# Two-layer hybrid attention trunk on Trainium2: in the last head of each attention, transposed blocks also go to the score tiles' PSUM places, some steps move from GpSimd to VectorE, and three groups of the second branch's projection are opened before the last gated rows are there

## The chip, the cores and the metric

The kernel runs on one core of a Trainium2 chip. Its five engines run their own instruction streams side by side and wait for each other through semaphores: TensorE (PE in the profile; PEld is its weight load), VectorE (DVE), ScalarE (ACT), GpSimd (POOL) and SyncE (SP), from whose queue the DMAs go out. The metric is device time in microseconds, the median of several executions. A profiled execution has its own time, the span from its first instruction to its last.

## The reference, cut to what matters

Two layers. Each normalises 512 latent and 256 context tokens of 1024 channels, projects them, runs two attentions of eight heads of 64 channels beside each other, multiplies each result by its own gate path, projects both to 1024 channels, merges them and projects again. Layer 0 also updates the 256 context tokens, layer 1 the 512 latent tokens alone.

```python
def _attend(q, k, v):
    s = jnp.einsum('bqkgd,btkd->bkgqt', q, k).astype(jnp.float32) * (HEAD_DIM ** -0.5)
    p = jax.nn.softmax(s, axis=-1).astype(v.dtype)
    return jnp.einsum('bkgqt,btkd->bqkgd', p, v)

def _merge(a_att, b_att, a_z, b_z, g_a, g_b, w_o_a, w_o_b, w_out):
    o_a = (a_att * jax.nn.silu(a_z)) @ w_o_a
    o_b = (b_att * jax.nn.silu(b_z)) @ w_o_b
    merged = jax.nn.sigmoid(g_a) * o_a + jax.nn.sigmoid(g_b) * o_b
    return merged @ w_out

# in _layer
    a_att = _na_latent(qa, ka, va, cka, cva, rpb, rows)   # neighbourhood window + all context keys
    b_att = _gqa_latent(qb, k_all, v_all)                 # all 768 keys, 2 key/value heads
    out_x = _merge(a_att, b_att, a_z, b_z, g_a, g_b, w_o_a, w_o_b, w_out)
    x_new = x + gate_x * out_x
```

## The kernel before

**Arithmetic.** Every product of two float32 matrices is made of three matmuls on a high and a low half of each operand (`mm3`, L339 to L343: high by high on L341, the two mixed ones on L342 and L343). A high half is a cast by ScalarE (`pth` L658, `gbh` L543, `whi`), a low half is the rest, left by a subtraction on VectorE or GpSimd (`ptl` L659, `gbl` L544, `wlo`).

**Stages.** Per layer: the projections of keys, queries, values and gates; the neighbourhood attention (NA); the gate path of the second branch; the grouped-query attention (GQ), and beside it, as filling work, the first branch's output projection (`o_a`); then the merge: the second branch's output projection (`o_b`, `w_o_b`) and the last projection with `w_out`. In layer 0 there are 768 tokens, in spans (0:512) and (512:768), in layer 1 only (0:512).

**One attention.** `pipeline` takes the heads in turn: the scores of head h, then the values of head h-1, then some pieces of the filling work. After the scores of head 7 it runs what is left of the filling work and `early`, and the values of head 7. Scores are a product into PSUM (`pss`), a maximum, an exponential on ScalarE, and a normalisation (`softmax_tail`) on GpSimd for tiles 1 and 3 of the four and on VectorE for tiles 0 and 2. The values of a head go block by block (six in GQ, four in NA): four 128x128 transposes of the probabilities into PSUM (`transpose_split`, L653 and L655, tile `pst`), the cast `pth` on ScalarE, the subtraction `ptl` on VectorE, and two or more matmuls into the one value tile `psv` (L807 to L818 in NA, L958 and L959 in GQ). `head_out` then copies and adds the halves of `psv` (`ho`, L667 on ScalarE, L668 on VectorE) and multiplies the gate path's tile by it on GpSimd (L669). In layer 0 a small value product of the context tokens follows each head (L732, L733, in a `psv` of its own).

**Places.** PSUM has two places `t` for transposed blocks (`pst`), one for a projection's sums (`psf`), and what is left depends on the stage: in NA three places `s` for scores (512 columns), in GQ two (1024 columns each), in both one place `v` for `psv`; in the merge five places `x` (`psx`). `pth` and `ptl` have two buffers each (`NT_NA = NT_GQ = 2`). A place is free again when its last reader is done, and the next instruction that writes it waits for that.

**The gated operand of `o_b`.** `zb` holds the gate path multiplied by the attention, four row blocks k = 0 to 3 of two heads each. `hilo(zb, gated["b"], ...)` (L540 to L544) splits them into `gbh` (ScalarE) and `gbl` (GpSimd). Blocks 0 to 2 are split in `early`, before the values of head 7, block 3 (heads 6 and 7) after the pool of the attention is closed. A group of `o_b` (128 output channels by one span of tokens) is four times three matmuls, k = 0 to 3, and its evacuation `evac_b` multiplies the sum by the merge gate (L993), adds (L994), casts (`mh`, L996) and subtracts (`ml`, L997). `gbh` and `gbl` share their large buffers with earlier tiles: in layer 0 `gbl` gets the buffer of `gal`, the low half of the first branch.

**What sets the order.** The program's text gives a first order; a scheduler with a timeline of its own reorders the instructions of each engine at build time, within the dependences. `behind(engine, fn)` ties the instructions of `fn` behind the last one issued so far on that engine.

## Time and profile before

| | |
|---|---|
| time, three runs | 1154.92 us median (1154.86 to 1157.67) |
| span of the profiled execution | 1153.4 us |
| busy: PE, PEld, DVE | 1123.0, 949.0, 809.8 us |
| busy: ACT, POOL | 573.9, 495.0 us |
| PE busy in 883.0 to 893.4 (end of NA, layer 1) | 8.94 of 10.40 us |
| PE busy in 1063.2 to 1084.6 (end of GQ, layer 1) | 18.63 of 21.40 us |
| PE busy in 560.3 to 570.1 (end of GQ, layer 0) | 7.81 of 9.80 us |

NA runs from about 150 to 305 us in layer 0 and from 780 to 893 us in layer 1; GQ from about 305 to 568 us and from 960 to 1084.6 us. The busy time of PE counts pipelined matmuls whose ends are modelled: two in a row start about 0.23 us apart at 512 columns and are listed with 0.39 us each. In a timeline each row is one instruction or several alike: its start, its length, the engine, the line, the operation, what it writes and reads, the tile, the shape, how many; in brackets the idle time ahead of it and what ended it.

### The profile page before, as it was taken

The numbers are of one execution on the slowest core, as the hardware profiler recorded it, in microseconds if no ns is written. First come the engines' busy times: TensorE is split into PE (matmuls) and PEld (weight loads), VectorE is DVE, ScalarE is ACT, GpSimd is POOL, SyncE is SP. The second block draws the span as 40 slices with busy tenths as digits, with TensorE's granted clock in tenths as the row PEclk, the third lists the DMA queues.
The fourth block names the chain that finished last, engine by engine and source line by source line (L and its number), as shares of the span: only waits on it lengthen the run. The fifth ranks groups of instructions, "written<-read, shape, count | busy, mean of one in ns | idle before, by whom it ended". The sixth has DMA issues, their size and how long they took to land.

```text
span 1153.4 us, 17280 instructions
## 1 busy us (share of the span) xinstructions
PE 1123.0 (97%) x6078; PEld 949.0 (82%) x6078; DVE 809.8 (70%) x1508; ACT 573.9 (50%) x1167; POOL 495.0 (43%) x459
## 2 busy tenths in 40 slices
PE   5999999999999999999999999999999999999998
PEld 4688888889988888878788787888888988887786
DVE  4566688897464687688587755469787665898563
ACT  5453266666433465566330265346666445766521
POOL 3362354454375243354411126245553664465311
PEclk9999999999999999999999999999999999999999
DMA  9644222233342332470353523543332333142143
GB/s 368 195 126 137 69 85 65 72 115 97 115 130 63 107 102 73 67 276 19 121 172 101 174 74 110 176 106 113 108 105 84 110 101 101 65 173 92 63 129 92
DMA packets 88000, 134.04 MB, mean 116 GB/s; under 512 B 10629, under 2 KB 52585, under 8 KB 86249
## 3 DMA queue, kind: packets, MB, share of 16 engines
q1 hardware_dynamic: 87912, 132.94, 36.8%
q8 instruction: 48, 0.79, 0.3%
q14 instruction: 40, 0.32, 0.1%
HBM read 115.58 MB, written 17.32 MB: 115 GB/s over the span
## 4 chain that ended last, share of the span: by engine, by line
PE 83%; DVE 7%; issue 3%; POOL 2%; ACT 2%; DMA 2%; ACTq 0%; POOLq 0%; DVEq 0%
PE psx L341 12%; PE psx L343 12%; PE psx L342 12%; PE psf L341 9%; PE psf L342 9%; PE psf L343 9%; PE pst L655 5%; PE pss L704 2%; PE pss L705 2%; PE psv L959 2%; PE psv L958 1%; PE pss L781 1%; PE pst L417 1%; DVE wlo L328 1%; DVE ptl L659 1%
## 5 line engine op out<-in xcount | busy, mean ns | idle before, releaser
L659 DVE TENSOR_TENSOR ptl<-pst,pth 128x512 fp32r<-128x512 f32 (+1 forms) x176 | 116.0, 672 | 46.4 <-ACT pth L658 45.4
L658 ACT CAST pth<-pst 128x512 fp32r<-128x512 f32 (+1 forms) x176 | 99.2, 576 | 87.5 <-PE pst L655 56.3
L328 POOL TENSOR_TENSOR wlo<-raw,whi 128x512 fp32r<-128x512 f32 x68 | 95.0, 1402 | 108.9 <-ACT whi L326 87.8
L341 PE MATMUL psf<-hx,whi 128*128 128x512 f32 (+1 forms) x368 | 139.2, 378 | 0.0
L342 PE MATMUL psf<-hx,whi 128*128 128x512 f32 (+1 forms) x368 | 138.1, 375 | 0.0
L343 PE MATMUL psf<-hx,wlo 128*128 128x512 f32 (+1 forms) x368 | 137.8, 374 | 0.0
L341 PE MATMUL psx<-whi,hx 128*128 128x512 f32 (+1 forms) x368 | 137.2, 374 | 0.0
L342 PE MATMUL psx<-wlo,hx 128*128 128x512 f32 (+1 forms) x368 | 135.8, 369 | 0.0
L343 PE MATMUL psx<-whi,hx 128*128 128x512 f32 (+1 forms) x368 | 133.6, 369 | 0.0
L314 POOL TENSOR_TENSOR wlo<-raw,whi 128x512 fp32r<-128x512 f32 x44 | 60.4, 1373 | 140.4 <-ACT whi L311 123.8
L311 ACT CAST whi<-raw 128x512 fp32r<-128x512 f32 x96 | 58.7, 623 | 103.5 <-PE psx L343 38.6
L326 ACT CAST whi<-raw 128x512 fp32r<-128x512 f32 x136 | 82.5, 622 | 50.3 <-DMA raw<-in_w_in_dram 34.1
L655 PE MATMUL pst<-ident,p 128*128 128x128 f32 x640 | 99.9, 272 | 1.4 <-DVE ptl L659 0.9
L328 DVE TENSOR_TENSOR wlo<-raw,whi 128x512 fp32r<-128x512 f32 x68 | 70.2, 1033 | 28.3 <-ACT whi L326 27.8
L655 PEld LDWEIGHTS pst<-ident,p 128*128 128x128 f32 x640 | 77.7, 141 | 13.3 <-DVE ptl L659 1.6
L644 POOL TENSOR_SCALAR r<-r 128x1 f32<-128x1 f32 x64 | 23.1, 361 | 151.7 <-DVE r L639 144.1
L645 POOL TENSOR_TENSOR p<-p,r 128x512 f32<-128x512 f32 (+1 forms) x64 | 83.5, 1304 | 5.0
L341 PEld LDWEIGHTS psx<-whi,hx 128*128 128x128 f32 x368 | 69.6, 189 | 11.8 <-issue 0.8
L343 PEld LDWEIGHTS psf<-hx,wlo 128*128 128x128 f32 x368 | 69.4, 188 | 11.8
L343 PEld LDWEIGHTS psx<-whi,hx 128*128 128x128 f32 x368 | 69.4, 189 | 11.5
L342 PEld LDWEIGHTS psx<-wlo,hx 128*128 128x128 f32 x368 | 69.6, 189 | 11.0
L341 PEld LDWEIGHTS psf<-hx,whi 128*128 128x128 f32 x368 | 69.4, 189 | 10.8 <-ACT zt L502 0.2
(239 smaller groups left out, 3033.4 us busy)
## 6 DMA issues: line engine op xcount, KB each, us to landing
raw<-in_w_in_dram SPq DMA_DIRECT2D x168, 256.0 KB, 2.9
rawb<-in_w_ada_dram SPq DMA_DIRECT2D x64, 256.0 KB, 2.8
gs<-zt SPq DMA_DIRECT2D x32, 256.0 KB, 2.0
raw<-in_w_out_dram SPq DMA_DIRECT2D x32, 256.0 KB, 2.8
tg<-gs SPq DMA_DIRECT2D x4, 1536.0 KB, 7.4
rawx<-in_w_ada_dram SPq DMA_DIRECT2D x4, 1024.0 KB, 7.2
rawy<-in_w_ada_dram SPq DMA_DIRECT2D x4, 1024.0 KB, 12.2
raw<-in_w_o_a_dram SPq DMA_DIRECT2D x16, 256.0 KB, 2.7
```

The source lines that it names most:

```text
L311: S.copy(hi[:, :n], raw[:, :n])
L314: e.tensor_tensor(lo[:, :n], raw[:, :n], F(hi[:, :n]), ALU.subtract)
L326: S.copy(hi, raw)
L328: lo_eng(i).tensor_tensor(lo, raw, F(hi), ALU.subtract)
L341: T.matmul(ps, lhs[0], rhs[0], start=first, stop=False)
L342: T.matmul(ps, lhs[0], rhs[1], start=False, stop=False)
L343: T.matmul(ps, lhs[1], rhs[0], start=False, stop=last)
L644: G.tensor_scalar(r[:, i:i + 1], r[:, i:i + 1], 0.5, None, ALU.mult)
L645: G.tensor_tensor(p[:, c0:c1], p[:, c0:c1], r[:, i:i + 1].to_broadcast([128, c1 - c0]), ALU.mult)
L655: T.transpose(pt[:, c0:c0 + 128], src, ident)
L658: S.copy(hi[:, n0:n1], pt[:, n0:n1])
L659: V.tensor_tensor(lo[:, n0:n1], pt[:, n0:n1], F(hi[:, n0:n1]), ALU.subtract)
```

## The change

Four edits, all at the end of an attention:

1. `att["end"]` is set ahead of the values of head 7. From then on every second transposed block goes into a score place `s` (so it is named `pss`) and its two halves into buffers of the probability tiles (`p`) in place of `pth` and `ptl`.
2. In the same stretch the last multiplication of `head_out` is on VectorE, and for head 7 the tiles normalised by GpSimd are 0 and 2 where they were 1 and 3 (`pooled`).
3. Within the pool of GQ, after the values of head 7, three groups of `o_b` are opened: the first in `psf`, two in the halves of one score place (`room`). Their matmuls for k = 0 to 2 are tied behind the last matmul of the values. Then `zb`'s block 3 is split, its low half on VectorE, and the three groups get k = 3 and `evac_b`. In layer 0 these groups are channels 0 (both spans) and 1 (first span), in layer 1 channels 0, 1 and 2.
4. The other groups follow in the merge's pool in the plain order of the loop, with their weights loaded two chunks ahead (`need_wb`) where `o_chunks` stood.

```diff
...
         ps = psw(n1 - n0)
-        nk = len(w)
-        for k in range(nk):
+        chan_mm(ps, w, f, a, n0, n1, 0, len(w))
+        evac(f, n0, n1, ps)
+
+    def chan_mm(ps, w, f, a, n0, n1, k0, k1):
+        for k in range(k0, k1):
             hi, lo = a(0, k), a(1, k)
             mm3(ps, (w[k][0][:, 128 * f:128 * f + 128], w[k][1][:, 128 * f:128 * f + 128]),
-                (R(hi[:, n0:n1]), R(lo[:, n0:n1])), k == 0, k == nk - 1)
-        evac(f, n0, n1, ps)
+                (R(hi[:, n0:n1]), R(lo[:, n0:n1])), k == 0, k == len(w) - 1)
 
...
 
-        def hilo(src, dst, fs):
+        def hilo(src, dst, fs, lo=G):
             sv = src.rearrange("p (f n) -> p f n", f=4)
...
                 S.copy(R(dst[0][:, f, :ntok]), sv[:, f, :ntok])
-                G.tensor_tensor(R(dst[1][:, f, :ntok]), sv[:, f, :ntok], dst[0][:, f, :ntok], ALU.subtract)
+                lo.tensor_tensor(R(dst[1][:, f, :ntok]), sv[:, f, :ntok], dst[0][:, f, :ntok], ALU.subtract)
 
...
 
-                pt = psw(512, "t")
+                spare = att["end"] and att["turn"] % 2 == 1
+                att["turn"] += 1
+                pt = psw(512, "s" if spare else "t")
                 for src, c0 in blocks:
...
                         T.transpose(pt[:, c0:c0 + 128], src, ident)
-                hi = att["p"].tile([128, 512], F32R, tag="pth", name=nm("pth"), bufs=att["nt"])
-                lo = att["p"].tile([128, 512], F32R, tag="ptl", name=nm("ptl"), bufs=att["nt"])
+                if spare:
+                    hi, lo = R(p_tile()[:, 0:512]), R(p_tile()[:, 0:512])
+                else:
+                    hi = att["p"].tile([128, 512], F32R, tag="pth", name=nm("pth"), bufs=att["nt"])
+                    lo = att["p"].tile([128, 512], F32R, tag="ptl", name=nm("ptl"), bufs=att["nt"])
                 S.copy(hi[:, n0:n1], pt[:, n0:n1])
...
                 V.tensor_tensor(t1[m:m + 64, :n], po[m:m + 64, :n], t1[m:m + 64, :n], ALU.add)
-                G.tensor_tensor(dst, dst, t1[m:m + 64, :n], ALU.mult)
+                (V if att["end"] else G).tensor_tensor(dst, dst, t1[m:m + 64, :n], ALU.mult)
 
...
 
+            def pooled(tiles):
+                return [i - 1 for i in tiles] if att["h"] == 7 else tiles
+
             def p_tile():
...
                 att["w"], att["np"], att["nt"] = width, n_p, n_t
+                att["end"], att["turn"] = False, 0
                 return st
...
                                  accum_out=r[:, 0:1])
-                    softmax_tail(p, 512, r[:, 0:1], [(0, 512)], G if i in NA_POOL else None)
+                    softmax_tail(p, 512, r[:, 0:1], [(0, 512)], G if i in pooled(NA_POOL) else None)
                     ps_.append(p)
...
                     att["bg"] = bg if h > 3 or pm["n"] == 1 else []
+                    att["h"] = h
                     st = scores_of(h)
...
                 run(bg, len(bg))
+                att["end"] = True
                 values_of(7, prev)
...
                     S.activation(p, pss, AF.Exp, bias=mx[:, 0:1], accum_out=r[:, 0:1])
-                    softmax_tail(p, 768, r[:, 0:1], [(0, 768)], G if i in GQ_POOL else None)
+                    softmax_tail(p, 768, r[:, 0:1], [(0, 768)], G if i in pooled(GQ_POOL) else None)
                     ps_.append(p)
...
             pipeline(fill, 8, gq_first, values_of(zb, gq_values), early, bg)
+            ob, wb, mg = [], {}, []
+            act_b = lambda part, k: gated["b"][part][:, k, :]
+
+            def need_wb(f):
+                for i in range(f // 2, min(f // 2 + 2, 4)):
+                    if i not in wb:
+                        wb[i] = load_w2(w_o_b[l], 256 * i, 4, mix_lo)
+
+            def evac_b(f, n0, n1, ps):
+                a, b = tg_part(0, f, n0, n1), tg_part(1, f, n0, n1)
+                V.scalar_tensor_tensor(b, b, 1.0, ps, ALU.add, ALU.mult)
+                V.tensor_tensor(a, a, b, ALU.add)
+                if f // 4 == len(mg):
+                    mg.append(hilo_tiles("m"))
+                hi, lo = [m[:, f % 4, n0:n1] for m in mg[f // 4]]
+                S.copy(R(hi), a)
+                V.tensor_tensor(R(lo), a, hi, ALU.subtract)
+            groups = [(f, n0, n1) for f in range(8) for n0, n1 in spans]
+            room = psw(1024, "s")
+            for (f, n0, n1), ps in zip(groups, (psw(), room[:, 0:512], room[:, 512:1024])):
+                need_wb(f)
+                ps = ps[:, :n1 - n0]
+                behind(ON_PE, lambda: chan_mm(ps, wb[f // 2], f % 2, act_b, n0, n1, 0, 3))
+                ob.append((f, n0, n1, ps))
+            hilo(zb, gated["b"], [3], V)
+            for f, n0, n1, ps in ob:
+                chan_mm(ps, wb[f // 2], f % 2, act_b, n0, n1, 3, 4)
+                evac_b(f, n0, n1, ps)
             gq_es.close()
...
                 nc.sync.dma_start(gv[:, v, :], src.to_broadcast([128, DM]))
-            hilo(zb, gated["b"], [3])
...
-            chunks = o_chunks("b", None, evac_b)
-            chunks[0][0]()
-            for i in range(4):
-                if i < 3:
-                    chunks[i + 1][0]()
-                if i % 2 == 0:
-                    mg.append(hilo_tiles("m"))
-                for piece in chunks[i][1]:
-                    piece()
+            for f, n0, n1 in groups[len(ob):]:
+                need_wb(f)
+                chan_proj(wb[f // 2], f % 2, act_b, n0, n1, lambda _, a, b, ps, f=f: evac_b(f, a, b, ps))
```

No matmul is added or removed: PE has 5769 instructions in the listed order before and after. VectorE has 8 more, GpSimd 8 fewer.

How the order moves at three places. First PE at the end of NA in layer 1; `psv_9420` are the values of head 6, `psv_9529` those of head 7, `p_9381` and the like its probabilities. Before:

```order
L653 MATMUL pst_9541<-ident,p_9381 128x2x64
L655 MATMUL pst_9541<-ident,p_9391 128x128
L655 MATMUL pst_9541<-ident,p_9402 128x128
L655 MATMUL pst_9541<-ident,p_9412 128x128
L653 MATMUL pst_9552<-ident,p_9381 128x2x64
L655 MATMUL pst_9552<-ident,p_9391 128x128 x2
L655 MATMUL pst_9552<-ident,p_9402 128x128
L807 MATMUL psv_9529<-pth_9535,va_1709_7711 128x512
L808 MATMUL psv_9529<-ptl_9536,va_1709_7711 128x512
L807 MATMUL psv_9529<-pth_9546,va_1709_7711 128x512
L808 MATMUL psv_9529<-ptl_9547,va_1709_7711 128x512
```

Now, where `pss_9540` and `pss_9564` are two of head 7's blocks and `pst_9442` is one of head 6's:

```order
L657 MATMUL pss_9540<-ident,p_9380 128x2x64
L659 MATMUL pss_9540<-ident,p_9391 128x128
L657 MATMUL pss_9564<-ident,p_9380 128x2x64
L659 MATMUL pss_9540<-ident,p_9401 128x128
L659 MATMUL pss_9564<-ident,p_9401 128x128
L659 MATMUL pss_9540<-ident,p_9412 128x128
L659 MATMUL pss_9564<-ident,p_9412 128x128 x2
L657 MATMUL pst_9442<-ident,p_9222 128x2x64
L659 MATMUL pst_9442<-ident,p_9232 128x128 x2
L659 MATMUL pst_9442<-ident,p_9243 128x128
```

Two of head 7's four blocks are transposed before head 6 has its last two; before, all four came after.

Second, PE at the end of GQ in layer 0; `psv_6264` are the values of head 7, `psf_6238` (earlier in the list before) is the last group of `o_a`, `psf_6393` and `psf_6354` are the first group of `o_b`. Before:

```order
L341 MATMUL psf_6393<-gbh_6256,whi_6369 128x512
L958 MATMUL psv_6264<-pth_6314,vb_3447 128x512
L342 MATMUL psf_6393<-gbl_6257,whi_6369 128x512
L343 MATMUL psf_6393<-gbh_6256,wlo_6371 128x512
L341 MATMUL psf_6393<-gbh_6256,whi_6369 128x512
L959 MATMUL psv_6264<-ptl_6315,vb_3447 128x512
L958 MATMUL psv_6264<-pth_6325,vb_3447 128x512
L655 MATMUL pst_6335<-ident,p_6086 128x128 x4
L959 MATMUL psv_6264<-ptl_6326,vb_3447 128x512
L342 MATMUL psf_6393<-gbl_6257,whi_6369 128x512
L343 MATMUL psf_6393<-gbh_6256,wlo_6371 128x512
L341 MATMUL psf_6393<-gbh_6256,whi_6375 128x512
```

Now:

```order
L342 MATMUL psf_6238<-gal_5523,whi_5980 128x256
L343 MATMUL psf_6238<-gah_5522,wlo_5982 128x256
L971 MATMUL psv_6264<-pth_6325,vb_3447 128x512
L972 MATMUL psv_6264<-ptl_6326,vb_3447 128x512
L739 MATMUL psv_6344<-p_6340,vb_3447 128x256
L740 MATMUL psv_6344<-p_6341,vb_3447 128x256
L739 MATMUL psv_6344<-p_6340,vb_3447 128x256
L740 MATMUL psv_6344<-p_6341,vb_3447 128x256
L341 MATMUL psf_6354<-gbh_6256,whi_6357 128x512
L342 MATMUL psf_6354<-gbl_6257,whi_6357 128x512
L343 MATMUL psf_6354<-gbh_6256,wlo_6359 128x512
```

The first `o_b` matmuls stood between head 7's values; now they stand behind all of them, and the last `o_a` group, which came ahead of four blocks of head 7, stands ahead of the last one. VectorE at the same place, from the evacuation of that last `o_a` group on:

```order
L580 SCALAR_TENSOR_TENSOR tg_5534<-tg_5534,psf_6238 128x256
L328 TENSOR_TENSOR wlo_6550<-raw_6546,whi_6548 128x512
L675 TENSOR_TENSOR ho_6331<-psv_6264,ho_6331 64x512
L676 TENSOR_TENSOR zb_4101<-zb_4101,ho_6331 64x512
L675 TENSOR_TENSOR ho_6349<-psv_6344,ho_6349 64x256
L676 TENSOR_TENSOR zb_4101<-zb_4101,ho_6349 64x256
L546 TENSOR_TENSOR gbl_6257<-zb_4101,gbh_6256 128x768
L1002 SCALAR_TENSOR_TENSOR tg_6252<-tg_6252,psf_6354 128x512
```

The first value tile's addition (`ho_6331`) stands behind that evacuation and a weight subtraction (`wlo_6550`); the two gate multiplications (`zb_4101`) and the low half (`gbl_6257`), which were on GpSimd, follow it.

Third, PE in layer 1, at the last product of block 3; `psf_11818`, and now `psf_11779`, is the first open sum. Before, after the values of head 7:

```order
L958 MATMUL psv_11708<-pth_11769,vb_9656 128x512
L959 MATMUL psv_11708<-ptl_11770,vb_9656 128x512
L341 MATMUL psx_11835<-gbh_11700,whi_11794 128x512
L342 MATMUL psx_11835<-gbl_11701,whi_11794 128x512
L343 MATMUL psx_11835<-gbh_11700,wlo_11796 128x512
L341 MATMUL psx_11835<-gbh_11700,whi_11794 128x512
L342 MATMUL psx_11835<-gbl_11701,whi_11794 128x512
L343 MATMUL psx_11835<-gbh_11700,wlo_11796 128x512
```

Now, after the k = 0 to 2 products of the three open sums:

```order
L341 MATMUL psf_11779<-gbh_11699,whi_11788 128x512
L341 MATMUL pss_11778<-gbh_11699,whi_11788 128x512
L342 MATMUL psf_11779<-gbl_11700,whi_11788 128x512
L343 MATMUL psf_11779<-gbh_11699,wlo_11790 128x512
L342 MATMUL pss_11778<-gbl_11700,whi_11788 128x512
L343 MATMUL pss_11778<-gbh_11699,wlo_11790 128x512
L341 MATMUL psf_11879<-gbh_11699,whi_11794 128x512
L342 MATMUL psf_11879<-gbl_11700,whi_11794 128x512
L343 MATMUL psf_11879<-gbh_11699,wlo_11796 128x512
L341 MATMUL psf_11879<-gbh_11699,whi_11794 128x512
```

Before, the values of head 7 are followed by other sums, each in a place of its own; now the fourth group, `psf_11879`, takes the same place as the first as soon as its sum is closed.

8 lines of the change are left out of this document (removed).

## Prediction

> **What bounds the kernel now.** I read the page first, then the table of what PE waited for, then the busy time by stretches, then the timelines of the stretches in which PE stands still. The page:
>
> ```profile
> PE 1123.0 (97%) x6078; PEld 949.0 (82%) x6078; DVE 809.8 (70%) x1508; ACT 573.9 (50%) x1167; POOL 495.0 (43%) x459
> ...
> PE   5999999999999999999999999999999999999998
> ...
> PEclk9999999999999999999999999999999999999999
> ...
> PE 83%; DVE 7%; issue 3%; POOL 2%; ACT 2%; DMA 2%; ACTq 0%; POOLq 0%; DVEq 0%
> ```
>
> PE is busy 97% of the span, its granted clock never falls under nine tenths after the start, and 83% of the chain of waits is PE. The work of PE is not changed: the change can only give or take time in which PE stands still. The table of what PE waited for (total us, times, longest) is led, after the start of the kernel, by waits that belong to the ends of the attentions:
>
> ```profile
> PE psv L959 <- DVE ptl L659: 2.0, 3, 1.5
> PE pst L653 <- DVE ptl L659: 1.5, 3, 0.8
> PE psx L341 <- DVE ho L668: 1.2, 1, 1.2
> ```
>
> They sum to 4.7 us. By stretches, the ends of NA in layer 1, of GQ in layer 1 and of GQ in layer 0 (the first pair of numbers is PE's busy time):
>
> ```profile
> 883.00:893.40 10.40, 8.94 (x55) 6.71 (x55) 6.89 (x12) 5.86 (x12) 3.82 (x4) 1.00 0.02 6
> 1063.20:1084.60 21.40, 18.63 (x98) 13.14 (x98) 13.60 (x20) 11.21 (x20) 9.21 (x8) 1.00 0.20 58
> 560.30:570.10 9.80, 7.81 (x45) 5.98 (x44) 5.21 (x7) 3.27 (x6) 8.79 (x6) 1.00 0.26 80
> ```
>
> PE idles 10.40 - 8.94 = 1.46, 21.40 - 18.63 = 2.77 and 9.80 - 7.81 = 1.99 us there, 6.2 us in all. That, 0.5% of the span, is about all that the change can win. A difference under 0.3% (3.5 us) is taken as no change, since a measurement of this kernel hardly tells it from none.
>
> **The change, end by end.** *NA, layer 1.* The timeline of PE:
>
> ```profile
> 883.15 0.27 PE L653 MATMUL pst<-ident,p 128*128 128x128 f32 x1
> 883.26 0.49 PE L655 MATMUL pst<-ident,p 128*128 128x128 f32 x3
> 884.59 0.33 PE L653 MATMUL pst<-ident,p 128*128 128x128 f32 x1 [0.84 <-DVE ptl L659]
> ...
> 889.44 0.33 PE L653 MATMUL pst<-ident,p 128*128 128x128 f32 x1 [0.27 <-DVE ptl L659]
> ...
> 893.11 0.39 PE L817 MATMUL psv<-ptl,va 128*128 128x256 f32 x1 [0.19 <-DVE ptl L659]
> ...
> 893.43 0.30 PE L341 MATMUL psx<-whi,hx 128*128 128x256 f32 x1
> ```
>
> A block of head 6 waits 0.84 us for a place that a `ptl` still reads; head 7's blocks wait 0.27, and their last products 0.19. VectorE has the reason:
>
> ```profile
> 890.05 0.69 DVE L659 TENSOR_TENSOR ptl<-pst,pth 128x512 fp32r<-128x512 f32 x1
> 891.29 0.62 DVE L659 TENSOR_TENSOR ptl<-pst,pth 128x448 fp32r<-128x448 f32 x1 [0.55 <-ACT pth L658]
> 892.43 0.62 DVE L659 TENSOR_TENSOR ptl<-pst,pth 128x448 fp32r<-128x448 f32 x1 [0.52 <-ACT pth L658]
> ```
>
> With two places, each subtraction follows a cast that follows four transposes that had to wait for the subtraction before: they start 1.24 and 1.14 us apart, with 0.62 to 0.69 us of work. With four places two of head 7's blocks are transposed in the 0.84 us wait (eight transposes, 0.11 us apart as at 883.15 and 883.26, are 0.87 us), and the four subtractions no longer wait in turn. From the other side, VectorE now does two of head 7's subtractions ahead of one of head 6's, which comes some 0.35 us later than it could. The stretch idles 1.46 us: the gain lies between 0 and 1.46, and I take 1.2, near the upper end, since the transposes that fill the wait are work that stood behind it.
>
> *GQ, layer 1.*
>
> ```profile
> 1065.14 0.50 PE L959 MATMUL psv<-ptl,vb 128*128 128x512 f32 x1 [1.54 <-DVE ptl L659]
> ...
> 1078.20 0.66 PE L655 MATMUL pst<-ident,p 128*128 128x128 f32 x4 [0.44 <-DVE ptl L659]
> ...
> 1084.24 0.50 PE L959 MATMUL psv<-ptl,vb 128*128 128x512 f32 x1 [0.22 <-DVE ptl L659]
> 1084.58 0.40 PE L341 MATMUL psx<-gbh,whi 128*128 128x512 f32 x1
> 1084.82 0.39 PE L342 MATMUL psx<-gbl,whi 128*128 128x512 f32 x1
> ...
> 1090.06 0.39 PE L341 MATMUL psf<-gbh,whi 128*128 128x512 f32 x1
> ```
>
> Head 7's last four blocks run from 1078.20 to 1084.58, 6.38 us. Between these rows PE has 12 products, which start 0.23 to 0.24 us apart where nothing waits (1084.58 and 1084.82), and 16 transposes: 12 x 0.23 + 16 x 0.11 = 4.5 us of work, 1.9 us lost. The wait of 1.54 us at 1065.14 belongs to head 6 and stays. The twice as many places take away what is lost, up to 1.9 us; two subtractions and head 6's `ho` addition still queue in a row on VectorE ahead of the second block, about 0.7 us, so I take 1.2. What follows was hidden before: after 1084.58 PE runs open sums without a gap until block 3 is split and k = 3 comes (1090.06), 5.5 us later. Now the three open sums cover the same chain with 27 products, 27 x 0.23 = 6.2 us, so opening them wins nothing in layer 1. Their evacuation is new. The first group's last product and VectorE's evacuations before:
>
> ```profile
> 1091.19 0.39 PE L343 MATMUL psf<-gbh,wlo 128*128 128x512 f32 x1
> ```
>
> ```profile
> 1091.62 0.69 DVE L993 SCALAR_TENSOR_TENSOR tg<-tg,psf 128x512 f32<-128x512 f32 x1 [0.24 <-PE psf L343]
> ...
> 1092.82 1.57 DVE L994 TENSOR_TENSOR tg<-tg,tg 128x512 f32<-128x512 f32 x1
> ...
> 1094.91 0.68 DVE L994 TENSOR_TENSOR tg<-tg,tg 128x512 f32<-128x512 f32 x1
> ```
>
> From the start of a sum's last product to the end of its evacuation it takes 1091.62 - 1091.19 + 0.69 = 1.12 us. The order puts the fourth group, `psf_11879`, into the same place behind two products of the second sum: PE has its own 0.23 and 2 x 0.23 to do, and waits 1.12 - 0.69 = 0.4 to 0.5 us. `psf_12061`, first of the last projection, waits in the same way for the fourth group's evacuation behind three products: 1.12 - 4 x 0.23 = 0.2 us. The first `psx` groups lie where `room` was and wait for its two evacuations, which stand behind a weight subtraction: I put 0.25 us. Together 0.95 us lost. Bounds for this end: a gain of 1.9 where the evacuations hide, a loss of 3 where they pile up (rival B). I take -1.2 + 0.95 = -0.25.
>
> *GQ, layer 0.* PE, GpSimd and VectorE before:
>
> ```profile
> 559.93 0.28 PE L342 MATMUL psf<-gal,whi 128*128 128x256 f32 x1
> ...
> 562.95 0.40 PE L341 MATMUL psf<-gbh,whi 128*128 128x512 f32 x1
> 563.34 0.50 PE L959 MATMUL psv<-ptl,vb 128*128 128x512 f32 x1
> ...
> 565.04 0.40 PE L341 MATMUL psf<-gbh,whi 128*128 128x512 f32 x1
> 566.22 0.50 PE L342 MATMUL psf<-gbl,whi 128*128 128x512 f32 x1 [0.79 <-POOL gbl L544]
> ...
> 568.22 0.28 PE L343 MATMUL psx<-gbh,wlo 128*128 128x256 f32 x1
> 569.70 0.50 PE L341 MATMUL psx<-gbh,whi 128*128 128x512 f32 x1 [1.20 <-DVE ho L668]
> ```
>
> ```profile
> 560.29 4.09 POOL L544 TENSOR_TENSOR gbl<-zb,gbh 128x768 fp32r<-128x768 f32 x2 [3.60 <-PE psf L342]
> ```
>
> ```profile
> 560.37 0.42 DVE L578 SCALAR_TENSOR_TENSOR tg<-tg,psf 128x256 f32<-128x256 f32 x1 [0.22 <-PE psf L343]
> 560.90 1.78 DVE L328 TENSOR_TENSOR wlo<-raw,whi 128x512 fp32r<-128x512 f32 x1
> ...
> 565.88 0.69 DVE L668 TENSOR_TENSOR ho<-psv,ho 64x512 f32<-64x512 f32 x1
> ```
>
> GpSimd does the three low halves `gbl` in one run of 5.87 us. It starts at 560.29, when the last `o_a` product with `gal`, whose buffer it takes, is through (started at 559.93). PE filled these 6.3 us (559.93 to the product at 566.22) with four blocks of head 7 and lost (563.34 - 562.95 - 0.23) + (566.22 - 565.04 - 0.23) = 0.16 + 0.95 us; at 569.70 it waits for the addition ahead of a place that `psv` held, 569.70 - 568.22 - 0.12 = 1.36 us. In all 2.5 us. In the new order the last `o_a` group stands behind all but one of head 7's blocks, so the same 5.87 us start with less to do. From that product on PE has: itself and one more of 256 columns (2 x 0.12), 2 products of the last block (0.46), 4 of the context (0.48), the six of k = 0 and 1 in the first open sum (1.38) and the first of k = 2 (0.23), 2.8 us; the low half of k = 2 comes after 6.3 us. PE stands 3.5 us. The context's products need `psv`, freed by VectorE behind an evacuation of 0.42 and a weight subtraction that takes 1.78 beside GpSimd: with the addition of 0.69 that is about 3.2 us, and the 2.1 us of products behind it still end before 6.3. The wait for the addition (1.36) is gone, since the open sums run meanwhile. The next group in `psf` waits for its evacuation: the same 1.12 us, of which two products of 256 columns and the last one's own step cover 0.4 to 0.5: 0.7. Another 0.1 at the first `psx`. That is 4.3 us against 2.5: a loss of 1.8. Bounds: a gain of 2.5 if GpSimd's run starts as early as before, a loss of 5 if nothing but the stretch behind the last block covers it.
>
> The moved multiplications and low halves (`zb`, `gbl` on VectorE) have no row on VectorE before. Nearest are the addition, 0.69 us, and the subtraction of two buffers beside GpSimd, 1.78; alone I take 0.69, nearest in shape. In layer 0 block 3 is ready some 8 us after the product of 559.93: the first addition at 3.2, the context's products 0.5, its copy, addition and multiplication at most 0.69 each, the cast and the low half of 768 columns 1.5 times 0.69 each. PE needs it at 6.3 + 0.5 (the rest of k = 2) + 9 x 0.12 + 9 x 0.23 (the other two sums) = 9.9 us. So these steps cost nothing with 1.9 us to spare, and 3 x 1.1 - 1.9 = 1.4 us if three of them take 1.78.
>
> *NA, layer 0.* Products of the projections stand between head 7's blocks there and cover them; I take 0, within half a microsecond either way. ScalarE's casts, the weight loads and the DMAs stay as many; the loads of `w_o_b` move ahead by one pool, where SP and ScalarE have room: 0.
>
> **Sum.** -1.2 - 0.25 + 1.8 + 0 = +0.35 us on a span of 1153.4. The median of the runs is 1.5 us over that span, so 1155.3 us.
>
> **Rivals.** *A, the waits go and none comes (faster).* The new order does what it is laid out for: layer 1's two ends lose their idle time, 1.46 + 2.77 = 4.2 us, and GQ in layer 0 comes out even, because GpSimd's run starts early enough. For it: nearly all of that idle time hangs on `ptl`, the very place that is doubled. Against it: 1.54 us are head 6's, and GpSimd's run is tied to the last `o_a` product, which the order sets back. Time 1154.9 - 4.2 = 1150.7.
>
> *B, VectorE beside GpSimd (slower).* The steps that move to VectorE read two buffers, and its evacuations now run while GpSimd makes weights. The subtraction of 1.78 us at 560.90 ran inside GpSimd's 5.87, the addition at 1092.82 took 1.57 where the one at 1094.91 took 0.68. If these steps pay 1 us each in the ends of both GQ: 1.4 us in layer 0 beyond the spare time, on top of the 1.8, and in layer 1 four evacuation steps ahead of the fourth group's (two additions, a weight, a low half), which make `psf_12061` wait 2 to 3 us. Sum 0.35 + 1.4 + 2.5 = 4.25 on top of 1154.9: 1159.2. It decides once more than two of these steps in a row meet GpSimd at work. The Trainium skill, "SBUF — State Buffer", section "Who interferes with whom", says that a VectorE instruction with two inputs in SBUF and a GpSimd one that reads SBUF share a read port, and one blocks the other. The trace agrees: 1.78 against 0.68 us, and no delay for the addition with one input in PSUM at 565.88, 0.69. By that rule every moved step is exposed, and the time would be B's.
>
> *C, the change does nothing.* The sums behind head 7 in layer 1 had no gap, and layer 0 might keep its old waits under new names: 1154.9.
>
> **How the numbers follow.** Forecast 0.44, A 0.25, B 0.25, C 0.06. The forecast's own range is 1153 to 1157.5; the range for 8 in 10 reaches into A and B, 1149.8 to 1160. Faster by over 0.3%: most of A and a little of the forecast, 0.25; slower: most of B and a little more, 0.26; within: 0.49.
>
> **What would show it.** Right: in layer 1 no wait of `psv` or `pst` for `ptl` over 0.2 us in head 7's blocks; a wait of 0.4 us or more of the fourth `psf` group; in layer 0 GpSimd's run of three `gbl` starting behind head 7's fifth block and 3 us or more of PE waits on it. Wrong: no wait on `gbl` in layer 0 (then A); VectorE's gate multiplications and low halves over 1.2 us and waits on them (B); a lower granted clock, or a new gap in the last projection, would put the result outside all three.

## The result, and the profile after

| | before | changed |
|---|---|---|
| time, median of five runs each | 1154.92 us (1154.51 to 1157.67) | 1159.49 us (1156.70 to 1160.60) |
| span of the profiled execution | 1153.4 us | 1157.5 us |
| ratio of the times, over all runs | | 1.0031, 95% interval 1.0018 to 1.0045 |

The changed kernel is slower by some 0.3% (the two medians alone differ by 0.4%); the profiled execution is 4.1 us longer. Its page, with the busy times and the shares of the chain that ended last:

```profile
span 1157.5 us, 17279 instructions
PE 1125.4 (97%) x6078; PEld 950.3 (82%) x6078; DVE 815.9 (70%) x1516; ACT 573.4 (50%) x1167; POOL 484.5 (42%) x451
...
PE 84%; DVE 8%; DMA 2%; ACT 2%; issue 1%; POOL 0%; DVEq 0%; ACTq 0%
```

PE is busy for 2.4 us more than before with the same matmuls (6078 records in both profiles; the 5769 given above is not their number), and the chain leads as before through PE. The longest waits of PE on an end of an attention (total us, times, longest):

```profile
PE psv L739 <- DVE ho L675: 2.6, 1, 2.6
PE psv L972 <- DVE ptl L666: 2.2, 4, 1.4
PE psf L341 <- DVE tg L1002: 1.1, 3, 0.6
...
PE psv L818 <- DVE ho L675: 1.0, 1, 1.0
```

`ptl` had led this table before; now it is the one value place: `psv` waits for the addition `ho` of `head_out`, L675, in three attentions (the third, 0.6 us at the end of GQ in layer 1, is shown below).

To see where the 4.1 us arose I compared the starts of the same instructions (same engine, operation and tiles) of ScalarE, VectorE and GpSimd in both traces: the median shift in a stretch, less that ahead of it. The start of the kernel, up to 140 us, which no edit touches, shifts by 0.5 us here and by 0 to 2 us from run to run, so it is kept apart.

| stretch | forecast | shift |
|---|---|---|
| start, untouched | 0 | +0.5 |
| NA, layer 0 | 0 | +0.1 |
| GQ, layer 0, with the merge | +1.8 | +3.4 |
| NA, layer 1 | -1.2 | -0.6 |
| GQ, layer 1, with the merge | -0.25 | +0.75 |
| sum | +0.35 | +4.1 |

**GQ, layer 0.** The timeline of PE from the last `o_a` product that reads `gal`:

```profile
563.18 0.28 PE L342 MATMUL psf<-gal,whi 128*128 128x256 f32 x1
...
563.65 0.39 PE L972 MATMUL psv<-ptl,vb 128*128 128x512 f32 x1
566.69 0.38 PE L739 MATMUL psv<-p,vb 128*128 128x256 f32 x1 [2.64 <-DVE ho L675]
...
567.44 0.63 PE L341 MATMUL psf<-gbh,whi 128*128 128x512 f32 x1
567.87 0.63 PE L342 MATMUL psf<-gbl,whi 128*128 128x512 f32 x1
...
570.43 0.39 PE L342 MATMUL psf<-gbl,whi 128*128 128x512 f32 x1
570.66 0.40 PE L343 MATMUL psf<-gbh,wlo 128*128 128x512 f32 x1
...
575.78 0.38 PE L341 MATMUL psf<-gbh,whi 128*128 128x256 f32 x1 [0.55 <-DVE tg L1002]
...
580.20 0.50 PE L341 MATMUL psx<-gbh,whi 128*128 128x512 f32 x1 [0.53 <-DVE tg L1002]
```

PE stands still for 2.64 us, waiting for the place of `psv`. Then the products start 0.43 us apart instead of 0.23, up to the one at 570.43. The granted clock is the last number but two in the busy time by stretches:

```profile
562.00:564.00 2.00, 2.00 (x15) 1.61 (x13) 0.38 (x1) 1.12 (x2) 0.46 (x1) 1.00 0.00 0
564.00:566.00 2.00, 0.05 (x1) 0.00 (x0) 1.86 (x3) 0.70 (x2) 2.00 (x2) 1.00 0.00 0
566.00:568.00 2.00, 1.31 (x6) 1.22 (x7) 1.97 (x2) 0.00 (x0) 2.00 (x2) 0.75 0.45 125
568.00:570.00 2.00, 2.00 (x6) 1.52 (x5) 1.48 (x3) 0.36 (x1) 2.00 (x2) 0.50 1.00 262
570.00:572.00 2.00, 2.00 (x14) 1.81 (x13) 1.10 (x2) 0.83 (x1) 1.25 (x1) 0.89 0.81 301
```

It is full until about 567.0, then half until about 570.4: half of the stretch 566 to 568 and 0.4 us of 570 to 572 give their 0.75 and 0.89. Meanwhile GpSimd does its run of three low halves, which begins right after the last `gal` product, as the order had made one expect:

```profile
563.54 6.27 POOL L546 TENSOR_TENSOR gbl<-zb,gbh 128x768 fp32r<-128x768 f32 x3 [3.96 <-PE psf L342]
```

It ends at 569.81; the third low half is used at 570.43, 0.6 us later and without a wait, since PE's products at half clock got there no earlier. VectorE in the same stretch:

```profile
564.15 1.75 DVE L328 TENSOR_TENSOR wlo<-raw,whi 128x512 fp32r<-128x512 f32 x1
565.94 0.69 DVE L675 TENSOR_TENSOR ho<-psv,ho 64x512 f32<-64x512 f32 x1
566.66 1.47 DVE L676 TENSOR_TENSOR zb<-zb,ho 64x512 f32<-64x512 f32 x1
```

The addition that frees `psv` stands behind a weight subtraction of 1.75 us, and the gate multiplication, new on VectorE, takes 1.47 us beside GpSimd. Block 3 is ready in time all the same. At 575.78 and 580.20 the first timeline has the waits for evacuations, 0.55 and 0.53 us.

**NA, layer 1.** In the ends of layer 1 no transposed block waits for a place any more, as here in NA:

```profile
893.02 0.39 PE L828 MATMUL psv<-ptl,va 128*128 128x256 f32 x1 [0.48 <-DVE ptl L666]
...
894.95 0.50 PE L818 MATMUL psv<-pth,va 128*128 128x512 f32 x1 [1.01 <-DVE ho L675]
```

In place of the 0.84 and 0.27 us on `ptl` that were there before, PE waits 1.01 us for the value place ahead of head 7's first product, and 0.48 us for a last `ptl` of head 6. The listed waits of this end come to as much as before (1.49 us after 1.30). The 0.6 us gained are in the starts: the excess of each start over the usual step, summed from before head 6's blocks to the end of NA, is 3.5 us where it was 4.1 (an estimate from the two timelines).

**GQ, layer 1.** PE's waits between 1055 and 1110 us:

```profile
PE psv L972 <- DVE ptl L666: 2.0, 3, 1.4
PE psv L971 <- DVE ho L675: 0.6, 1, 0.6
PE psf L341 <- DVE tg L1002: 0.5, 2, 0.3
```

Before:

```profile
PE psv L959 <- DVE ptl L659: 1.8, 2, 1.5
PE pst L655 <- DVE ptl L659: 0.9, 2, 0.4
```

The two places for transposed blocks are no longer waited for, the subtraction itself and the value place still are, and 0.5 us of waits for evacuations are new. The wait of 1.4 us, and that of 1.54 us at 1065.14 before, stand among the values of head 5 (by the additions `ho`, which come one a head), not of head 6 as the prediction has it.

### The profile page after: what moved, and what is told of

Read it like the earlier page. It is cut to its first block, busy times and chain, and to the rows that moved or that the text cites. A ratio compares the mean times of both kernels' runs of the same rounds, so it can differ in the third digit from the quotient of the medians.

```text
span 1157.5 us, 17279 instructions
## 1 busy us (share of the span) xinstructions
PE 1125.4 (97%) x6078; PEld 950.3 (82%) x6078; DVE 815.9 (70%) x1516; ACT 573.4 (50%) x1167; POOL 484.5 (42%) x451
## 4 chain that ended last, share of the span: by engine, by line
PE 84%; DVE 8%; DMA 2%; ACT 2%; issue 1%; POOL 0%; DVEq 0%; ACTq 0%
PE psx L343 12%; PE psx L341 12%; PE psx L342 12%; PE psf L341 10%; PE psf L342 9%; PE psf L343 9%; PE pst L659 4%; PE pss L711 2%; PE pss L712 2%; PE pss L792 2%; PE psv L972 2%; PE psv L971 1%; PE pst L419 1%; DVE ptl L666 1%; DVE wlo L328 1%
## 5 line engine op out<-in xcount | busy, mean ns | idle before, releaser
L341 PE MATMUL psx<-whi,hx 128*128 128x512 f32 (+1 forms) x376 | 140.6, 376 | 0.0
L342 PE MATMUL psx<-wlo,hx 128*128 128x512 f32 (+1 forms) x376 | 139.0, 370 | 0.0
L343 PE MATMUL psx<-whi,hx 128*128 128x512 f32 (+1 forms) x376 | 137.1, 371 | 0.0
L665 ACT CAST pth<-pst 128x512 fp32r<-128x512 f32 (+1 forms) x164 | 92.5, 576 | 74.4 <-PE pst L659 46.3
L666 DVE TENSOR_TENSOR ptl<-pst,pth 128x512 fp32r<-128x512 f32 (+1 forms) x164 | 108.0, 671 | 30.0 <-ACT pth L665 29.0
L659 PE MATMUL pst<-ident,p 128*128 128x128 f32 x596 | 92.6, 272 | 0.6 <-DVE r L641 0.6
L659 PEld LDWEIGHTS pst<-ident,p 128*128 128x128 f32 x596 | 72.3, 140 | 10.6 <-PE psv L740 0.7
L343 PEld LDWEIGHTS psx<-whi,hx 128*128 128x128 f32 x376 | 71.1, 189 | 12.0
L341 PEld LDWEIGHTS psx<-whi,hx 128*128 128x128 f32 x376 | 71.1, 189 | 12.0 <-issue 0.8
```

The source lines that it names most:

```text
L341: T.matmul(ps, lhs[0], rhs[0], start=first, stop=False)
L342: T.matmul(ps, lhs[0], rhs[1], start=False, stop=False)
L343: T.matmul(ps, lhs[1], rhs[0], start=False, stop=last)
L659: T.transpose(pt[:, c0:c0 + 128], src, ident)
L665: S.copy(hi[:, n0:n1], pt[:, n0:n1])
L666: V.tensor_tensor(lo[:, n0:n1], pt[:, n0:n1], F(hi[:, n0:n1]), ALU.subtract)
```

## The experiments

All were profiled once, on three chips, each time beside the kernel before (whose time was 1155.17, 1156.24 and 1156.13 us there). The table has the shift against the profile of before shown above in each stretch, worked out as above, in us; the start is taken with NA of layer 0. The one kernel that was profiled twice, no_open_sums and no_open_timed, agrees with itself to about 0.5 in the stretches behind the start. A kernel called "without edit 3" has the whole tail of before, so edit 4 is gone too, but the low half of block 3 stays on VectorE (except in no_open_gpsimd). Edit 4 was not tried by itself.

| kernel | start | GQ 0 | NA 1 | GQ 1 | span |
|---|---|---|---|---|---|
| changed | +0.6 | +3.4 | -0.6 | +0.75 | 1157.5 |
| ctx_other_place | +1.2 | +2.8 | -0.4 | +0.7 | 1157.6 |
| no_spare_places | +0.65 | +3.8 | +0.5 | +3.2 | 1163.0 |
| no_open_sums | +0.3 | -0.9 | -0.5 | -2.4 | 1149.9 |
| moves_back_to_gpsimd | -0.1 | +6.0 | -0.4 | +1.1 | 1160.0 |
| open_sums_untied | -0.2 | +1.8 | +1.15 | +3.7 | 1159.9 |
| open_sums_alone | 0 | +1.8 | 0 | +3.0 | 1158.2 |
| no_open_low_half_split | +1.9 | +1.0 | -0.4 | -2.4 | 1153.4 |
| no_open_gpsimd | +0.3 | +4.5 | -0.4 | -2.05 | 1155.7 |
| first_sum_free | 0 | +1.4 | -0.5 | -1.3 | 1152.9 |
| no_open_timed | +2.0 | -0.35 | -0.5 | -2.4 | 1152.2 |
| no_open_ctx_place | +0.4 | -1.7 | -0.5 | -2.4 | 1149.3 |
| no_open_old_tiles | +0.65 | +0.6 | -0.8 | -2.0 | 1151.8 |

no_spare_places loses another 1.5 us at the start of NA in layer 1, where PE waits for a maximum of the scores; the cause of that is open.

**The place of the value tile, or GpSimd's run?**

```diff
-                po = psw(256, "v")
+                po = psw(256, "t" if att["end"] else "v")
```

> The changed kernel, with the context's value product of head 7 in a place t (both attentions). Theory 1: in layer 0's GQ the price is the one value place and what follows the idle time (2.81 us of standing still for the addition of head 7, then some 4 us at half clock). Then the clock stays full at 560 to 580 us, and the end of that stretch comes 2.5 us or more earlier: span 1155 or less. Theory 2: GpSimd's run of three low halves ends at the same time anyway, and the wait for the place and the slow clock lie inside it. Then PE waits two or three times for gbl instead, the clock stays full, and the stretch gains 0.7 us at most: span 1156.8 to 1157.5.

The context's products moved ahead of the last `o_a` group. What PE then waited for, and the clock (again the last number but two):

```profile
566.41 0.50 PE L342 MATMUL psf<-gbl,whi 128*128 128x512 f32 x1 [0.83 <-POOL gbl L546]
...
568.63 0.50 PE L342 MATMUL psf<-gbl,whi 128*128 128x512 f32 x1 [1.26 <-POOL gbl L546]
...
570.86 0.50 PE L342 MATMUL psf<-gbl,whi 128*128 128x512 f32 x1 [1.27 <-POOL gbl L546]
```

```profile
566.00:568.00 2.00, 0.96 (x3) 0.49 (x3) 1.94 (x3) 0.00 (x0) 2.00 (x2) 1.00 0.10 7
568.00:570.00 2.00, 0.96 (x3) 0.49 (x3) 1.55 (x2) 0.36 (x1) 2.00 (x2) 1.00 0.89 282
```

Three waits for `gbl`, 3.4 us, a full clock, and a stretch only 0.6 us shorter: theory 2. The wait for the place and all but 0.6 us of the half clock lay inside GpSimd's run in the changed kernel. This holds for its order of PE's products, in which the first open sum's product of k = 2 stands ahead of the other two sums; the next runs show another order. (The half clock that the expectation puts at some 4 us lasted 3.4.)

**Which edit is the loss?** First without the spare places:

```diff
-                spare = att["end"] and att["turn"] % 2 == 1
+                spare = False
```

> The changed kernel without edit 1 (transposed blocks only in the places t). If the spare places brought the gain in the layer 1 ends, NA there goes back to the stalls of before (about 0.5 us more) and GQ there by about 0.3 us. In layer 0's GQ more of head 7's blocks stand behind the last o_a product, so GpSimd's run starts earlier against PE's work: by theory 1 and 2 the stretch gains 1.5 to 2.5 us. Span about 1156. If instead the spare places help everywhere, the span rises over 1158.

Layer 1 lost 1.1 us in NA where 0.5 was expected, and 2.4 us in GQ where it was 0.3, and layer 0's GQ gained nothing, though the last `o_a` product stood there ahead of four blocks of head 7 again (at 560.67 us), as in the kernel before: the span rose to 1163.0. The spare places are worth more than I had thought. Then without the open sums, with the tail of before:

```diff
-            ob, wb, mg = [], {}, []
...
-                chan_mm(ps, wb[f // 2], f % 2, act_b, n0, n1, 3, 4)
-                evac_b(f, n0, n1, ps)
...
+            hilo(zb, gated["b"], [3], V)
...
+            chunks = o_chunks("b", None, evac_b)
```

> The changed kernel without edit 3 (the open sums; the tail of the second projection as before, the low half of block 3 on VectorE). In layer 1 the two waits on the evacuations of the first sums (0.49 and 0.35 us) go: 0.8 us. In layer 0 products of the first group can run ahead of the context's, so PE stands still in shorter pieces: if an idle time of over 2 us is what lowers the clock, it stays full there, and the stretch gains 1 us or more; if GpSimd's run binds, it gains 0.6 at most. Span 1155 by the first, 1156.5 by the second.

The span fell to 1149.9, 3.5 us under the kernel before: both stretches of GQ gained far more than either theory had said, 4.3 us in layer 0 and 3.2 in layer 1. PE's waits between 1055 and 1110 us, and the place in the timeline where the changed kernel waited 1.40 us for a `ptl` of head 5:

```profile
PE psv L972 <- DVE ptl L666: 0.4, 2, 0.2
PE psv L971 <- DVE ho L675: 0.3, 1, 0.3
```

```profile
1062.04 0.48 PE L341 MATMUL psf<-gbh,whi 128*128 128x512 f32 x1
...
1062.80 0.50 PE L342 MATMUL psf<-gbl,whi 128*128 128x512 f32 x1
1063.14 0.39 PE L343 MATMUL psf<-gbh,wlo 128*128 128x512 f32 x1
1063.37 0.40 PE L341 MATMUL psf<-gbh,whi 128*128 128x512 f32 x1
...
1063.95 0.50 PE L972 MATMUL psv<-ptl,vb 128*128 128x512 f32 x1 [0.19 <-DVE ptl L666]
```

Products of the first open sum (`gbh`, `gbl` into `psf`) stand between head 5's values, and the wait is 0.19 us. The kernel before has such products there and among head 6's values too, nine in all, though only one of them ahead of its wait of 1.54 us:

```profile
1062.87 0.48 PE L341 MATMUL psf<-gbh,whi 128*128 128x512 f32 x1
...
1066.73 0.48 PE L342 MATMUL psf<-gbl,whi 128*128 128x512 f32 x1
1067.05 0.39 PE L343 MATMUL psf<-gbh,wlo 128*128 128x512 f32 x1
1067.28 0.40 PE L341 MATMUL psf<-gbh,whi 128*128 128x512 f32 x1
```

In the changed kernel they are tied behind head 7's last value product, and nothing of `o_b` is left to put between the values.

In layer 0 this run has the last `o_a` product set back just as far as the changed kernel, with one block of head 7 behind it, and a run of GpSimd just as long:

```profile
562.82 0.28 PE L342 MATMUL psf<-gal,whi 128*128 128x256 f32 x1
...
565.07 0.50 PE L342 MATMUL psf<-gbl,whi 128*128 128x512 f32 x1 [0.83 <-POOL gbl L546]
...
567.30 0.50 PE L342 MATMUL psf<-gbl,whi 128*128 128x512 f32 x1 [0.22 <-POOL gbl L546]
...
572.76 0.39 PE L342 MATMUL psf<-gbl,whi 128*128 128x512 f32 x1
```

```profile
563.19 6.32 POOL L546 TENSOR_TENSOR gbl<-zb,gbh 128x768 fp32r<-128x768 f32 x3 [3.94 <-PE psf L342]
```

Yet the stretch is 0.9 us shorter than before. PE waits 0.83, 0.31 (for `psv`) and 0.22 us, at full clock, and never for the third low half: from 568.1 on it has products of k = 0 and 1 for the groups in `psx`, and the first group's product of k = 2 comes at 572.76. So the set-back alone does not cost what the prediction asked for it.

Then the steps moved to VectorE:

```diff
-                (V if att["end"] else G).tensor_tensor(dst, dst, t1[m:m + 64, :n], ALU.mult)
+                G.tensor_tensor(dst, dst, t1[m:m + 64, :n], ALU.mult)
...
-            hilo(zb, gated["b"], [3], V)
+            hilo(zb, gated["b"], [3])
```

> The changed kernel with the multiplications of head 7 and the low half of block 3 back on GpSimd (edit 2 but for the softmax tiles). Rival B says that these steps beside GpSimd are the loss: then layer 0's GQ gains over 1 us. My reading is that they are off PE's path in both layers: the span stays within 0.7 us of the changed kernel's 1157.5, and in layer 0 GpSimd's queue makes block 3 later, which may cost up to 1 us.

Another 2.6 us lost in layer 0's GQ, where at most 1 was expected: block 3 came late, with 1.27 us of waiting for its low half and a second stretch of 3.4 us at half clock. Rival B's mechanism is not the loss, though one of its prices is real (1.47 us for a multiplication).

**The tie.**

```diff
-                behind(ON_PE, lambda: chan_mm(ps, wb[f // 2], f % 2, act_b, n0, n1, 0, 3))
+                chan_mm(ps, wb[f // 2], f % 2, act_b, n0, n1, 0, 3)
```

> The changed kernel with the three open sums as they are, but not tied behind the last value product (the call of behind is taken away). Theory 3: the tie is the loss, because the products of blocks k = 0 to 2 stood between the values of heads 6 and 7 and filled PE's waits for ptl there. Then layer 1's GQ gets back most of 2.2 us (the 1.67 us wait of head 6's values goes), layer 0's GQ 1 to 3 us, and what is left of the loss against the kernel without open sums is the evacuation waits of 0.8 us in layer 1 and 1.3 in layer 0: span 1152 to 1154. Theory 4: the places are the loss (evacuations of psf and room late, sums that take a score place): then the span stays over 1156.

Layer 0 gained 1.6 us, as expected, layer 1 lost 3: theory 3 as I had put it fails. The products went ahead and filled PE's waits among the values (of heads 5 and 6, not 6 and 7), and then there were none left for the time in which block 3 is split. After head 7's last value product:

```profile
1088.47 0.40 PE L972 MATMUL psv<-p,vb 128*128 128x512 f32 x1
1091.69 0.79 PE L341 MATMUL psf<-gbh,whi 128*128 128x512 f32 x1 [2.82 <-ACT gbh L545]
1092.28 0.63 PE L341 MATMUL pss<-gbh,whi 128*128 128x512 f32 x1
1092.71 0.63 PE L342 MATMUL psf<-gbl,whi 128*128 128x512 f32 x1
```

PE waits 2.82 us for `gbh`, and half clock follows, for 6.8 us. (The +1.15 in this run's NA is half clock too, with products 0.43 us apart at 892 to 894 us.)

**The open sums by themselves.**

```diff
-                spare = att["end"] and att["turn"] % 2 == 1
+                spare = False
...
-                return [i - 1 for i in tiles] if att["h"] == 7 else tiles
+                return tiles
...
-                (V if att["end"] else G).tensor_tensor(dst, dst, t1[m:m + 64, :n], ALU.mult)
+                G.tensor_tensor(dst, dst, t1[m:m + 64, :n], ALU.mult)
```

> The kernel before with edit 3 alone (open sums tied as in the change, block 3's low half on VectorE; no spare places, multiplications and softmax tiles as before). If edit 3 is the loss by itself it costs 6 us or more here too: span 1159 or more. If it only costs together with the spare places, which pull head 7's blocks ahead, the span is 1155 at most.

Edit 3 costs by itself, 1.8 us in layer 0 and 3.0 in layer 1, 4.8 where 6 or more were expected. In layer 1 the parts add up: -2.4 without it, +3.0 alone, +0.75 together. The 3.0 are, as an estimate, the nine products that stood between the values, 9 x 0.23 = 2.1 us, which now follow where nothing waits for them, and the 0.84 us of evacuations. In layer 0 the parts do not add up: -0.9 without it, +1.8 alone (there the last `o_a` product stands where it stood before, with four blocks behind it), +3.4 together. The longest idle time is 1.90 us here and 2.64 in the changed kernel, and the clock stays full here; a stretch of 3.4 us at half clock is, as an estimate, up to 1.7 us of the difference.

**Three open sums for two uses.** Theory 5, formed after these: the first sum free, the two in `room` tied (issued ahead of it, so that the tie holds them behind the values alone).

```diff
-            for (f, n0, n1), ps in zip(groups, (psw(), room[:, 0:512], room[:, 512:1024])):
+            for (f, n0, n1), ps in [*zip(groups, (psw(), room[:, 0:512], room[:, 512:1024]))][::-1]:
...
-                behind(ON_PE, lambda: chan_mm(ps, wb[f // 2], f % 2, act_b, n0, n1, 0, 3))
+                open_sum = lambda: chan_mm(ps, wb[f // 2], f % 2, act_b, n0, n1, 0, 3)
+                behind(ON_PE, open_sum) if len(ob) < 2 else open_sum()
                 ob.append((f, n0, n1, ps))
+            ob.reverse()
```

> The changed kernel with the two sums of room tied behind the values as they are and the first sum, in psf, free to move ahead. Theory 5: PE's products of blocks k = 0 to 2 have two uses, filling the waits for ptl between the values and covering the splitting of block 3 after them, and three open sums have products for one of the two; tied they only cover (waits 5.0 us among the values of layer 1's GQ), untied they only fill (2.99 us of waiting for block 3 after the values). Then nine free products fill and eighteen tied ones (4.1 us) cover, and what is left against the kernel without edit 3 is the wait for evacuations, 0.84 us: layer 1's GQ 1.2 to 1.8 us shorter than before, layer 0's within 1 us of before; span 1151.5 to 1153. By theory 4 (the places and late evacuations) the span stays over 1156.

Layer 1: -1.3 us, as expected, where the changed kernel has +0.75 and the untied one +3.7. The 2.05 us got back agree with the nine products' 2.1. There is no wait for block 3, and the two waits for evacuations (0.33 and 0.19 us, 0.84 us by the starts) are what is left against the kernel without edit 3, 1.1 us. Layer 0 came out at +1.4, 0.4 us over what was expected. Theory 4 would have had over 1156; the span is 1152.9. In the kernel before, the merge's five `psx` places were open for such sums already, beside `psf`: nine products in `psf` fill, and those in `psx` cover.

**Towards a faster kernel.** Five runs start from the kernel without edit 3. One splits the low halves of layer 0:

```diff
-                hilo(zb, gated["b"], range(3))
+                for f in range(3):
+                    hilo(zb, gated["b"], [f], V if first and f == 1 else G)
```

> The kernel without edit 3 (span 1149.9), and in layer 0 the second of the three low halves on VectorE, so that GpSimd's run is two and not three. PE's waits there were 1.10 and 0.39 us for gbl and 0.47 for the place of psv. If GpSimd's run sets the end of layer 0's GQ, 0.5 to 1.3 us go: span 1148.6 to 1149.4 but for 0.5 us of the start. If VectorE's own queue takes its place (the context's addition stands behind the low half), nothing is gained or up to 1 us lost.

Not gained: 1.0 us over before in that stretch, 1.9 over the kernel without edit 3, where a loss of up to 1 was expected. VectorE's queue came to be waited for (0.80 us for an evacuation ahead of the first `o_b` product), with half clock behind it; how much is due to which stays open.

One has the steps of edit 2 back on GpSimd, with the diff of moves_back_to_gpsimd.

> The kernel without edit 3, with the last multiplications of head 7 and block 3's low half back on GpSimd too; left of the change are the spare places and the softmax tiles. If the move to VectorE is worth something by itself, 0.5 to 2 us are lost against 1149.9, in layer 0's GQ above all, where block 3 comes later. If the gain is of the spare places alone, the span is within 0.5 us of 1149.9.

With the steps on GpSimd the stretch has +4.5 us, with them on VectorE -0.9; layer 1 differs by 0.35. The move to VectorE is worth more than was expected, in layer 0, where GpSimd is in its run of low halves. How much more stays open: the clock is half from 569.5 to 576.4 there, which at half speed is up to 3.4 of the 5.4 us, and the waits that came anew are 0.81 us for `gbl` and 0.56 for `ho`.

One has the softmax tiles of before for head 7:

```diff
-                return [i - 1 for i in tiles] if att["h"] == 7 else tiles
+                return tiles
```

> The kernel without edit 3, with head 7's softmax on the tiles of before (GpSimd tiles 1 and 3). If the order of the tiles matters it is in the first transposes of head 7: up to 0.5 us lost in each NA. I expect no difference over 0.5 us anywhere.

0.4 us lost in layer 1's GQ, 1.5 in layer 0's, where the waits were those of the kernel without edit 3 (0.83, 0.31 and 0.21 us) but half clock followed them this once; no difference over 0.5 was expected.

The last two were timed: the kernel without edit 3 as it was, and with the diff of ctx_other_place.

> The kernel without edit 3, with the context's value product of head 7 in a place t. In layer 0's GQ the 0.47 us wait for the place of psv goes, and open sums of the next groups stand between the low halves and take up 0.3 to 0.8 us of the waits for gbl: span 1149 to 1149.7, time 0.05 to 0.1% under the kernel without edit 3. If GpSimd's run alone sets this end, no difference.

> The kernel without edit 3 once more, timed: 0.2 to 0.4% faster than the kernel before if the one look (span 1149.9 against 1153.4) holds; the same if that look was only a run in which the clock did not fall.

Timed side by side with the kernel before (median 1156.13 us, 13 runs): the kernel without edit 3 has 1152.84 us (6 runs), the one with the context's product in a place t 1152.82 (7 runs); both ratios are 0.9971, interval 0.9960 to 0.9982. So edits 1 and 2, with block 3's low half on VectorE, make the kernel 0.3% faster than before, as expected, and 0.6% lies between that and the change as a whole. The second one's stretch in layer 0 is 0.8 to 1.3 us shorter in the profiles, but the times don't tell the two apart.

## Why the prediction was right, and where not

The time, 1159.5 us, lies in the range (1149.8 to 1160) near its upper end; 1155.3 was forecast, and the forecast's own range ended at 1157.5. That the wide range held is luck in part: it reached so far up for rival B, whose mechanism the runs refute. A loss was forecast in layer 0 and gains in layer 1; the loss came, nearly twice as large, and of the gains only half of the one in NA, which GQ gave back. Three terms came out too fast.

*Layer 0's GQ: +1.8 forecast, +3.4 measured.* The order came as forecast: the last `o_a` product set back, GpSimd's run starting behind it and behind head 7's fifth block, PE out of work. Two sizes were off. "PE stands 3.5 us": from the product of 563.18 to the one at 570.43 it is 7.25 us and not 6.3, 0.4 of it since the run took 6.27 us and not 5.87, the rest for the slow clock. And the evacuation waits after it were 0.72 and 0.70 us by the starts, where I had 0.7 and 0.1. "That is about 3.2 us" for the addition that frees `psv` was near: it ended 565.94 + 0.69 - 563.18 = 3.45 us after that product. What such a wait does to the clock was not in the sum. The cause was wrong: I put the loss down to the set-back of the last `o_a` product. no_open_sums has the same set-back, and its stretch is 0.9 us shorter than before; open_sums_alone and no_spare_places have no set-back and lose 1.8 and 3.8. It is edit 3 that leaves PE short of products during GpSimd's run: 1.6 us of the loss go with the tie alone (open_sums_untied, at full clock), and 1.4 are the waits for evacuations. How the rest is shared out is not shown.

*The signs.* Those for layer 1 came (the wait of the fourth `psf` group is 0.49 us by the starts), and so did GpSimd's run behind head 7's fifth block, but not the 3 us of waits on it: PE waited 2.64 us for `ho` and not at all for `gbl`. No wait on `gbl` was named as a sign of rival A, which did not come either. A lower granted clock, which was to put the result outside all three, came for 3.4 us and left it inside the range.

*Layer 1's GQ: -0.25 forecast, +0.75 measured.* "I put 0.25 us" and the 0.4 to 0.5 and 0.2 for the evacuations: 0.49 and 0.35 us by the starts, 0.84 against 0.95, right. The step that failed is the one ahead: "opening them wins nothing in layer 1". It loses there, because the tie takes the nine products, 2.1 us, from among the values of heads 5 and 6. So "I take 1.2" for the values came to 0.1 (0.84 of evacuations, 0.75 in all); without the edit the stretch gains 2.4. I had the products in view (the order shows the first sum's last product alone behind the values) and priced only what the open sums cover, not where their work had stood. "The wait of 1.54 us at 1065.14 belongs to head 6 and stays": it is head 5's, and it stays (1.40 us) only where the sums are tied; without edit 3 it is 0.19.

*Layer 1's NA: -1.2 forecast, -0.6 measured.* The waits on `ptl` went, as argued. "Near the upper end" was wrong: they were replaced by the next wait in line, 1.01 us for the one value place, which is free only when VectorE has added head 6's halves. A wait for a place that was hidden behind another place was not among my costs.

*Layer 0's NA: 0 forecast, +0.1 measured.* Right.

*The rivals.* A, that the waits of layer 1 go, is what edits 1 and 2 do when edit 3 is taken away: -2.9 us there by no_open_sums, against 4.2 in the rival. B gave nearly the measured time, 1159.2, by another mechanism: its gate multiplication does take 1.47 us where 0.69 was the price alone, but PE does not wait for it, and by moves_back_to_gpsimd the moved steps still gain. In layer 1, where B has 2 to 3 us of piled-up evacuations, the additions of the first ones took 0.68 us and PE lost 0.84 in all. The Trainium skill's "SBUF — State Buffer", section "Who interferes with whom", agrees with those rows again: the multiplication with both inputs in SBUF took 1.47 us beside GpSimd's run, the addition with an input in PSUM 0.69.

## What to carry to other kernels

Work that an engine could do early has two uses, to fill waits ahead of a dependence and to cover the latency behind it; tying it to the one takes it from the other, so ask where its instructions stood before pricing what they cover. A place that is doubled hands the wait on to the next single place (here the value tile), so price that one too. Where a long run on another engine starts on the release of a buffer, moving the last reader back need not bring the run into the open: here it cost nothing where PE had other products for that time. So list what the engine can do during the run before pricing it.

## What the runs showed of the hardware

After PE had stood still for 2.64 us in the changed kernel its granted clock was half for 3.4 us (567.0 to 570.4: products of 512 columns 0.43 us apart); after 2.82 us in open_sums_untied it was half for 6.8 us (1090.8 to 1097.6). Three waits of 0.83 to 1.27 us with work between them left it full in ctx_other_place, but waits that no_open_sums got through at full clock (0.83, 0.31, 0.22 us) were followed by half clock in no_open_old_tiles: idle time alone doesn't decide it. In all the profiles, each stretch at one clock, but for the first and the last of a run, is 3.41 us long or a multiple of it. In the 3.41 us ahead of a slow stretch PE was busy for 0.76 us (changed kernel), 1.5 (open_sums_untied, 1087.4 to 1090.8), 1.8 (no_open_low_half_split, 564.5 to 567.9) and 2.1 us (no_open_old_tiles, 563.7 to 567.1), while 3.41 us with 1.8 us of work (ctx_other_place, 566.1 to 569.5; open_sums_alone, 565.0 to 568.5) were followed by full clock. So this busy time, as the profile counts it, doesn't fully decide it either.

The Trainium skill, "TensorE: Matmul & The Clock Gate", Part 1, tells of a free-running window of about 3.4 us by which the clock is halved when idle and restored when busy, and of 427 ns from one product of 512 columns to the next at half clock. The 0.43 us, the 3.4 us and the different outcome of like waits agree with it; that a whole idle window is needed does not, since 2.64 us of idle time were enough.

Of the changed kernel's five runs the one with a granted clock of 1.000 took 1156.7 us, the four at 0.995 to 0.997 took 1159.3 to 1160.6, so about 3 us of a single run's time may hang on it. In the 13 runs of the kernel before that were timed with the last two experiments, no such tie shows: 1156.25 us at 0.996, 1156.08 at 0.999.
